# Sums of weight blocks made ahead: twenty sets instead of thirteen, and five of eight pairs as sums in every gate and up product

## The chip, the cores and the metric

One NeuronCore of a Trainium2 chip runs the whole program. The time is the device time of one execution in microseconds (us); less is better. The engines are TensorE (PE; its weight loads are listed as PEld), VectorE (DVE), ScalarE (ACT), GpSimd (POOL) and SyncE (SP, which only issues transfers). Transfers (DMA) move data between HBM and the on-chip memory SBUF, or from HBM to HBM.

## The reference

One layer of an encoder on x (256 tokens x 2048) and mem (256 x 2048), all in f32:

```python
h = rms_norm(x, g_mix); proj = h @ w_in                 # latents for one attention, q/k/v for the other
x = x + concat(out_mla, out_diff) @ w_out               # two kinds of attention heads
hx, hm = rms_norm(x, g_xattn), rms_norm(mem, g_mem)
xo = attention(hx @ w_xq, hm @ w_xk, hm @ w_xv)         # 4 heads into mem
x = x + xo @ w_xo
hf = rms_norm(x, g_ffn)
x = x + (silu(hf @ w_gate) * (hf @ w_up)) @ w_down      # hidden width 5632
return rms_norm(x, g_final)
```

The change concerns the two products hf @ w_gate and hf @ w_up, whose weights have 2048 rows and 5632 columns each.

## The kernel before, in words

**Products.** f32 operands are split in a high part (rounded to fp32r, a cast on ACT) and a low part (the rest, a subtraction on DVE), `split_into`. A product of a 128-row block with 512 columns of weights is three matmuls: high by high, high by low, low by high (`mm`, `mm_late`). Activations (256 tokens, two halves of 128) are the stationary operand, weights the moving one.

**Pairs.** In the wide products (w_out, gate, up, down; `wide_project`) the weights come in pairs: 256 rows by 1024 columns, four blocks of 128 x 512, 1 MB. A pair of kind "P" is used plainly: 8 products, 24 matmuls. A pair of kind "W" is used as sums in Strassen-Winograd fashion, 7 products, 21 matmuls. For that, sums of the activations' blocks are made once (`summed_pair`, the "forms"), and four sums of the weight blocks are needed for each pair: with the blocks stored in the order b0, b1, b2, b3 they are t1 = b1 + b0, t3 = b2 + b0, t2 = t1 + b2, t4 = t2 + b3. Each needed block or sum is split on ACT and DVE. Without sums made ahead, DVE makes the four where they are used (tiles tsum, tsum2). Strings such as 'PPWPWPWW' say the kind of each of the eight pairs of a product, and a tuple beside it the order in which they are used; the third item names a block whose low part is made by an accumulating transfer instead of DVE ("carried").

**Early sets.** `ahead()` is called once for each piece of weights in the projections and pairs before the feed-forward part, and counts these calls as steps: from 0 in the projections of the second attention, through w_out (from 20), the cross-attention (from 36) and w_xo (48 to 51), on into the feed-forward part. An entry ((chunk, 0 for gate or 1 for up, pair), step, own) of `AHEAD` makes the four sums of that pair at that step: two loads of the blocks by SP, four additions on DVE, two stores of the sums to HBM by POOL. With own = 0 the two tiles are taken from the pool act, with own = 1 from a pool of their own (apart). Later `wide_project` finds the set in `made`, loads three of the pair's four raw blocks and the four sums (tile tmade, 1 MB, one buffer), and DVE has no sums to make for that pair.

**Feed-forward part.** A first narrow chunk of 512 columns of gate and up together, then five chunks of 1024 columns; each is a gate product, then an up product (`wide_chunk`), each of eight pairs. After the narrow chunk and chunk 0, after chunks 1 and 2, and after 3 and 4 the down projection of what is there follows (`wide_add`).

**Order.** Every operation is recorded and then ordered by a planner (`Plan.emit`), with a cost for each kind (`Plan.cost`: time on the engine, lag to the result, time of the transfer). It runs its own model of the engines and the transfer queue, derives from it a latest start for each operation, and writes each engine's instructions out in the modelled order. On the chip each engine goes through its list in order and waits by semaphores. An operation's lag may be raised by hand (`.lag += 6.5`), which lets what depends on it come later in the lists. All operations are issued by one helper line, so the profile gives line 244 for all; tiles tell them apart. `wraw` is a raw pair of weights, `wh` and `wl` its split parts, `ahead` the tiles of early sets, `sums` their places in HBM, `acc` and `q` PSUM accumulators.

Of the kernel before, what the change touches and what calls it, by code (L numbers as in the profile page):

```python
# [10 lines left out]
F32 = mybir.dt.float32  # L11
# [4 lines left out]
ALU = mybir.AluOpType  # L16
AX = mybir.AxisListType

P = 128
# [20 lines left out]

NARROW_KINDS, NARROW_ORDER = "PPWPWPPP", (0, 1, 3, 2, 5, 4, 6, 7)
GATE_UP = [
    (('PPWPWPWW', (0, 2, 1, 4, 3, 6, 7, 5), ((0, 1),)),
     ('PPWWWPWW', (0, 2, 3, 1, 4, 6, 7, 5), ((0, 1),))),
    (('PPWPWPWW', (0, 2, 1, 4, 3, 6, 7, 5), ((0, 1),)),
     ('PPWWWPWW', (0, 2, 3, 1, 4, 6, 7, 5), ((0, 1),))),
    (('PPWWWPWW', (0, 2, 3, 1, 4, 6, 7, 5), ((0, 1),)),
     ('PPWWWPWW', (0, 2, 3, 1, 4, 6, 7, 5), ((0, 1),))),
    (('PPWPWPWW', (0, 2, 1, 4, 3, 6, 7, 5), ((0, 1),)),
     ('PPWWWPWW', (0, 2, 3, 1, 4, 6, 7, 5), ((0, 1),))),  # L50
    (('PPWWWPWW', (0, 2, 3, 1, 4, 6, 7, 5), ((0, 1),)),
     ('PPWWWPWW', (0, 2, 3, 1, 4, 6, 7, 5), ((0, 1),))),
]
X2_KINDS = "".join("W" if "W" in k else "P" for k in zip(NARROW_KINDS, *[p[0] for c in GATE_UP for p in c]))

AHEAD = (((0, 1, 2), 2, 0), ((0, 1, 6), 6, 1), ((1, 1, 2), 9, 0), ((1, 1, 6), 11, 0), ((2, 1, 2), 14, 0), ((2, 1, 6), 39, 1), ((3, 1, 2), 40, 0), ((3, 1, 6), 46, 0), ((4, 1, 2), 46, 0), ((4, 1, 6), 46, 1), ((4, 0, 6), 49, 0), ((2, 0, 6), 49, 0), ((4, 0, 2), 50, 0))

OUT_KINDS, OUT_ORDERS = ("PPPPWWWP", "PPPPWWWP"), ((0, 1, 2, 3, 4, 5, 7, 6), (0, 1, 2, 4, 3, 5, 7, 6))  # L60

# [136 lines left out]
class Plan:  # L198
# [64 lines left out]

    def cost(self, engine, method, out, ins, kw):
        if kw.get("accum_op") is not None:
            return 0.6, 4.5, 2.8
        if method == "dma_start":
            size = max(x.cols() for x in out + ins) * 512
            return {"gpsimd": 0.55, "sync": 0.45, "scalar": 0.45}[engine], 2.0 + size / 375e3, size / 381e3
        n = max([x.cols() for x in out[:1]] + ([x.cols() for x in ins[:1]] if "reduce" in method else []))  # L270
        in_psum = bool(ins) and ins[0].tile.whole
        if engine == "tensor":
            t = 0.108 if method == "transpose" else 0.0134 + n / 2400
            return t, t + 0.14, 0.0
        if engine == "gpsimd":
            if method in ("memset", "affine_select", "tensor_copy"):
                t = 0.1 + n * 1.2e-3
            else:
                t = 1.0 if n <= 2 else 1.2
            return t, t + 0.03, 0.0  # L280
        if engine == "vector":
            if n <= 16 and "reduce" not in method:
                t = 0.08
            elif method == "scalar_tensor_tensor":
                t = 0.127 + n * 1.05e-3
            elif method == "tensor_scalar":
                t = 0.129 + n * 1.035e-3 if in_psum else n / 960
            elif method == "tensor_tensor_reduce":
                t = 0.145 + n / 960
            elif method == "tensor_copy":  # L290
                t = n / 960
            else:
                t = 0.068 + n / 960
            return t, t + 0.082, 0.0
        t = 0.044 + 0.855e-3 * n if in_psum else 0.092 + 0.842e-3 * n
        if isinstance(kw.get("scale"), Ref) or isinstance(kw.get("bias"), Ref):
            t += 0.09 if n < 512 else 0.15
        if kw.get("accum_out") is not None:
            t += 0.093
        return t, t + (0.15 if kw.get("accum_out") is not None else 0.08), 0.0  # L300
# [171 lines left out]
def encoder_block(tc: tile.TileContext, a, out):  # L472
    nc = plan = Plan(tc)
# [42 lines left out]
    def act_tile(shape=(P, 4, S), name="act"):  # L516
        return Split(
            act.tile(list(shape), F32R, name=name + "_h", tag="act"),
            act.tile(list(shape), F32R, name=name + "_l", tag="act"),
        )  # L520
# [37 lines left out]
    def project(actT, pieces, before=None, fine=0):  # L558

        accs = [acc_tile() for _ in range(NT)]  # L560
        ncols = pieces[0].shape[2]
        nk = sum(src.shape[1] for src in pieces)
        kt = 0
        for i, src in enumerate(pieces):
            if before is not None:
                before(i)
            ahead()
            for w in weights(src, i < fine):
                x = actT(kt)
                for tt in range(NT):  # L570
                    mm(accs[tt][:, :ncols], x[tt] if isinstance(x, tuple) else x[:, tt * P:(tt + 1) * P], w,
                       start=kt == 0, stop=kt == nk - 1)
                kt += 1
        return accs
# [4 lines left out]
    def nat(name):  # L579
        pool, bufs = nat_pool  # L580
        return pool.tile([P, 512], F32, name=name, tag="nat", bufs=bufs)
# [27 lines left out]
    dram = plan.pool("dram", 1, bass.MemoryType.DRAM)  # L609
    made, steps = {}, [None]  # L610

    def ahead():

        if steps[0] is None:
            return
        for key, at, own in AHEAD:
            if at != steps[0]:
                continue
            src = a[("w_gate", "w_up")[key[1]]][key[0], key[2]]
            x, y = [pool.tile([P, 2, 512], F32, name="ahead", tag=tag)  # L620
                    for pool, tag in ((apart, "ahead" + n) if own else (act, "act") for n in "xy")]
            nc.sync.dma_start(out=x, in_=src[:, 1:3, :]).lag += 6.5
            nc.sync.dma_start(out=y, in_=src[:, 0:4:3, :]).lag += 6.5
            made[key] = d = dram.tile([P, 4, 512], F32, name="sums%d_%d_%d" % key)
            nc.vector.tensor_tensor(out=x[:, 0, :], in0=x[:, 0, :], in1=y[:, 0, :], op=ALU.add)
            nc.vector.tensor_tensor(out=y[:, 0, :], in0=x[:, 1, :], in1=y[:, 0, :], op=ALU.add)
            nc.vector.tensor_tensor(out=x[:, 1, :], in0=x[:, 0, :], in1=x[:, 1, :], op=ALU.add)
            nc.gpsimd.dma_start(out=d[:, 0:4:2, :], in_=x).lag += 3.5
            nc.vector.tensor_tensor(out=y[:, 1, :], in0=x[:, 1, :], in1=y[:, 1, :], op=ALU.add)
            nc.gpsimd.dma_start(out=d[:, 1:4:2, :], in_=y).lag += 3.5  # L630
        steps[0] += 1

    def pair_raw(src, part=False):
# [55 lines left out]
    def wide_project(pairs, src, order, kinds, leave, join, closed=(0, 1), before=None, seed=None, carried=(), sums={}):  # L689
# [6 lines left out]
        for n, i in enumerate(order):  # L696
            stop = n == len(order) - 1
            if before is not None:
                before(n)
            ahead()  # L700
            d = sums.get(i)
            raw = pair_raw(src[i], d is not None)
            if d is not None:
                t = sum_pool[0].tile([P, 4, 512], F32, name="tmade", tag="tmade", bufs=1)
                nc.sync.dma_start(out=t, in_=d).lag += 2.5
            if n == 0 and seed is not None:
                loaded = plan.ops[-1]
                for tt in range(NT):
# [23 lines left out]
            elif sum_pool:  # L732
                t = sum_pool[0].tile([P, 2, 512], F32, name="tsum", tag="tsum", bufs=1)
# [8 lines left out]
            else:  # L742
                b21 = split_blocks(raw[:, 3:4, :])
                t = [soft.tile([P, 512], F32, name="tsum", tag="e", bufs=4) for _ in range(4)]
# [10 lines left out]
            own = i == summed[0], i == summed[-1]  # L755
# [15 lines left out]
    def wide_result(pairs, src, order, kinds, carried=(), sums={}):  # L771

        res = []

        def leave(Q):
            res[:] = [act.tile([P, 2, 512], F32, name=f"res{tt}", tag="act") for tt in range(NT)]
            q1, x, v, y = res[0][:, 0, :], res[0][:, 1, :], res[1][:, 0, :], res[1][:, 1, :]
            nc.scalar.copy(out=q1, in_=Q[1])
            nc.vector.tensor_tensor(out=v, in0=Q[6], in1=q1, op=ALU.subtract)
            nc.vector.tensor_tensor(out=x, in0=Q[5], in1=v, op=ALU.add)  # L780
            nc.vector.tensor_tensor(out=v, in0=v, in1=Q[7], op=ALU.subtract)
            nc.vector.tensor_tensor(out=y, in0=Q[5], in1=v, op=ALU.add)

        def join(tt, oc, acc):
            r = res[tt][:, oc, :]
            nc.vector.tensor_tensor(out=r, in0=acc, in1=r, op=ALU.subtract if (tt, oc) == (1, 0) else ALU.add)

        wide_project(pairs, src, order, kinds, leave, join, carried=carried, sums=sums)
        return res
# [87 lines left out]
    for i in range(8):  # L877
# [8 lines left out]
        for k, w in enumerate(weights(a["w_in_lat"][i], one_by_one,  # L886
# [3 lines left out]
            for tt in range(NT):  # L890
                x = xk[:, tt * P:(tt + 1) * P]
# [227 lines left out]
    for hg in range(2):  # L1119
        t = act_tile(name="mixT")  # L1120
# [141 lines left out]
    for tt in range(NT):  # L1262
        n = nat("xk")
# [6 lines left out]
    for tt in range(NT):  # L1270
        n = nat("xq")
# [19 lines left out]
    for oc in range(4):  # L1291
# [7 lines left out]
        for n in range(2):  # L1299
# [6 lines left out]
            if not plain:  # L1306
                t = act_tile(name="x2T")
# [60 lines left out]
    for gi, (chunks, order) in enumerate(groups):  # L1368
# [6 lines left out]
        src = [a["w_dn"][h, pair0:pair0 + len(hp)] for h in range(2)]  # L1375
# [149 lines left out]
```

## Time and profile before

| | |
|---|---|
| median of 3 runs | 1129.36 us (1128.56 to 1129.73) |
| the profiled execution | 1129.81 us, span 1128.0 us from first to last instruction |
| mean granted TensorE clock | 0.998 |
| early sets: additions on DVE | 52 of 0.68 us (13 sets) |
| loads of made sums (tmade) | 13 of 1 MB |
| bytes moved | 267.53 MB, mean 237 GB/s |

A page of the profile is one execution. Busy shares are averages over the whole span; a matmul that overlaps the next counts as busy, so PE at 99% is read together with the number of matmuls in a stretch. A wait is put down to the event that ended it. In the chain that ended last each row has start, duration and what ran or was waited for. The feed-forward part takes about the second half and more of the span.

### The profile page before, as it was taken

How to read it: one execution, taken by the hardware profiler on the slowest of the kernel's cores; microseconds unless marked ns; L12 is line 12 of the kernel's file. 1: busy time of each engine (PE TensorE's matmuls, PEld its weight loads, DVE VectorE, ACT ScalarE, POOL GpSimd, SP SyncE). 2: the span in 40 equal slices, each digit the busy share in tenths (PEclk: the TensorE clock that was granted, in tenths of full speed). 3: DMA queues.
4: the chain of work that ended last, by engine and by line, in shares of the span. 5: the costliest groups of instructions: out<-in, count | busy, mean ns of one | idle time of the engine just before them, and what ended most of it. 6: DMA issues, size and time to landing. Idle time of an engine off the chain costs nothing.

```text
span 1128.0 us, 14989 instructions
## 1 busy us (share of the span) xinstructions
PE 1117.4 (99%) x5328; PEld 934.3 (83%) x5328; DVE 1040.1 (92%) x1429; ACT 726.0 (64%) x1030; POOL 90.3 (8%) x116
## 2 busy tenths in 40 slices
PE   9999999999999999999999999999999999999997
PEld 7889888888888888888888888888878888888886
DVE  7798889779999899999999999999989999999995
ACT  7756455467775556657776576777656576767752
POOL 5830001000001010000000000000000000000000
PEclk9999999999999999999999999999999999999999
DMA  9745577647676995659657686686566776777543
GB/s 357 261 161 191 187 279 251 240 168 266 234 285 222 360 388 217 206 200 305 223 191 244 219 278 206 247 282 224 189 206 212 257 258 233 279 250 232 219 149 113
DMA packets 48683, 267.53 MB, mean 237 GB/s; under 512 B 5601, under 2 KB 6881, under 8 KB 24289
## 3 DMA queue, kind: packets, MB, share of 16 engines
q1 hardware_dynamic: 40976, 240.46, 59.2%
q0 software_dynamic: 6768, 24.64, 7.4%
q10 hardware_dynamic: 864, 1.47, 0.4%
q8 instruction: 42, 0.69, 0.2%
q14 instruction: 33, 0.26, 0.1%
HBM read 242.96 MB, written 15.73 MB: 229 GB/s over the span
## 4 chain that ended last, share of the span: by engine, by line
PE 93%; DVE 3%; DMA 2%; issue 1%; ACT 0%; SPq 0%; POOLq 0%; POOL 0%; DVEq 0%; ACTq 0%
PE acc L244 69%; PE q L244 16%; PE pt L244 2%; PE psc L244 2%; PE acckv L244 1%; DMA ahead<-in_w_gate 1%; DVE wl L244 1%; PE qT L244 1%; DMA wl<-wraw 1%; PE po L244 1%; PE kT L244 1%; PE pod L244 1%; PE ppt L244 0%; PE wps L244 0%; DVE tsum L244 0%
## 5 line engine op out<-in xcount | busy, mean ns | idle before, releaser
L244 ACT CAST wh<-wraw 128x1024 fp32r<-128x1024 f32 (+2 forms) x401 | 384.1, 967 | 237.3 <-PE acc L244 182.6
L244 DVE TENSOR_TENSOR wl<-wraw,wh 128x1024 fp32r<-128x1024 f32 (+2 forms) x386 | 426.7, 1116 | 51.1 <-ACT wh L244 46.6
L244 ACT CAST wh<-tsum 128x1024 fp32r<-128x1024 f32 (+1 forms) x112 | 112.0, 1005 | 48.8 <-PE acc L244 25.5
L244 DVE TENSOR_TENSOR wl<-tsum,wh 128x1024 fp32r<-128x1024 f32 (+1 forms) x112 | 129.7, 1161 | 3.7 <-ACT wh L244 2.0
L244 PE MATMUL q<-wh,forms_h 128*128 128x512 f32 x270 | 105.5, 391 | 0.2 <-DVE hT_l L244 0.2
L244 PE MATMUL q<-wh,forms_l 128*128 128x512 f32 x270 | 105.5, 391 | 0.0
L244 PE MATMUL acc<-wh,forms_h 128*128 128x512 f32 x261 | 101.9, 391 | 0.0
L244 PE MATMUL acc<-wh,forms_l 128*128 128x512 f32 x261 | 101.6, 389 | 0.0
L244 PE MATMUL acc<-wl,forms_h 128*128 128x512 f32 x261 | 94.8, 389 | 0.0
L244 PE MATMUL q<-wl,forms_h 128*128 128x512 f32 x270 | 93.9, 389 | 0.0
L244 PE MATMUL acc<-wh,x0T_h 128*128 128x512 f32 x224 | 88.6, 397 | 0.0
L244 PE MATMUL acc<-wh,x0T_l 128*128 128x512 f32 x224 | 88.4, 395 | 0.0
L244 PE MATMUL acc<-wl,x0T_h 128*128 128x512 f32 x224 | 87.9, 393 | 0.0
L244 DVE TENSOR_TENSOR tsum<-tsum,wraw 128x512 f32<-128x512 f32 x112 | 76.6, 684 | 0.7
L244 PE MATMUL acc<-wh,hT_l 128*128 128x512 f32 x188 | 73.4, 390 | 0.0
L244 PE MATMUL acc<-wh,hT_h 128*128 128x512 f32 x188 | 73.4, 390 | 0.0
L244 DVE TENSOR_TENSOR tsum<-wraw 128x1024 f32<-128x1024 f32 (+1 forms) x62 | 68.8, 1114 | 3.8 <-DMA wraw<-in_w_dn 2.5
L244 PE MATMUL acc<-wh,x2T_l 128*128 128x512 f32 x176 | 68.7, 390 | 0.0
L244 PE MATMUL acc<-wh,x2T_h 128*128 128x512 f32 x176 | 68.7, 390 | 0.0
L244 PEld LDWEIGHTS q<-wh,forms_h 128*128 128x128 f32 x270 | 50.7, 188 | 11.3 <-DVE hT_l L244 0.9
L244 PEld LDWEIGHTS q<-wl,forms_h 128*128 128x128 f32 x270 | 50.7, 188 | 10.6
L244 PEld LDWEIGHTS q<-wh,forms_l 128*128 128x128 f32 x270 | 50.7, 188 | 10.2
(375 smaller groups left out, 2319.4 us busy)
## 6 DMA issues: line engine op xcount, KB each, us to landing
wraw<-in_w_dn SPq DMA_DIRECT2D x41, 1024.0 KB, 4.7
wraw<-in_w_gate SPq DMA_DIRECT2D x37, 1024.0 KB, 4.8
wraw<-in_w_up SPq DMA_DIRECT2D x30, 1024.0 KB, 5.2
wraw<-in_w_in SPq DMA_DIRECT2D x24, 1024.0 KB, 5.3
wraw<-in_w_out SPq DMA_DIRECT2D x16, 1024.0 KB, 4.8
sums<-ahead POOLq DMA_DIRECT2D x26, 512.0 KB, 7.5
tmade<-sums SPq DMA_DIRECT2D x13, 1024.0 KB, 6.6
ahead<-in_w_up SPq DMA_DIRECT2D x20, 512.0 KB, 7.8
```

The costliest lines, as they stand in the source:

```text
L244: getattr(getattr(self.tc.nc, engine), method)(*[made(x) for x in args], **{k: made(x) for k, x in kw.items()})
```

## The change

Gate takes five of its eight pairs as sums in all five chunks (before: four in chunks 0, 1 and 3). The early sets grow from thirteen to twenty, so that pairs 2 and 6 of every gate and up product are made ahead, and are spread over steps 3 to 50. Six of them (own = 2) are made without SBUF and DVE: SP copies four blocks from HBM to HBM, and POOL issues four accumulating transfers that add the other blocks. The planner's cost of an accumulating transfer now goes by its size (for the size used before it stays as it was), and the lags of early loads, stores and of the loads of made sums are raised.

```diff
 GATE_UP = [
-    (('PPWPWPWW', (0, 2, 1, 4, 3, 6, 7, 5), ((0, 1),)),
-     ('PPWWWPWW', (0, 2, 3, 1, 4, 6, 7, 5), ((0, 1),))),
...
     (('PPWWWPWW', (0, 2, 3, 1, 4, 6, 7, 5), ((0, 1),)),
      ('PPWWWPWW', (0, 2, 3, 1, 4, 6, 7, 5), ((0, 1),))),
...
+] * 5
-AHEAD = (((0, 1, 2), 2, 0), ((0, 1, 6), 6, 1), ((1, 1, 2), 9, 0), ((1, 1, 6), 11, 0), ((2, 1, 2), 14, 0), ((2, 1, 6), 39, 1), ((3, 1, 2), 40, 0), ((3, 1, 6), 46, 0), ((4, 1, 2), 46, 0), ((4, 1, 6), 46, 1), ((4, 0, 6), 49, 0), ((2, 0, 6), 49, 0), ((4, 0, 2), 50, 0))
+AHEAD = (((0, 1, 2), 3, 1), ((0, 1, 6), 5, 0), ((1, 1, 2), 7, 0), ((1, 1, 6), 10, 0), ((2, 1, 2), 11, 2), ((2, 1, 6), 13, 0), ((3, 1, 2), 16, 1), ((3, 1, 6), 18, 0), ((4, 1, 2), 18, 2), ((4, 1, 6), 21, 0), ((4, 0, 6), 30, 2), ((2, 0, 6), 34, 2), ((4, 0, 2), 38, 2), ((0, 0, 6), 40, 2), ((3, 0, 6), 42, 0), ((2, 0, 2), 43, 1), ((1, 0, 6), 47, 0), ((3, 0, 2), 47, 0), ((0, 0, 2), 50, 0), ((1, 0, 2), 50, 0))
...
         if kw.get("accum_op") is not None:
-            return 0.6, 4.5, 2.8
+            size = out[0].cols() * 512
+            return 0.6, 1.7 + size / 188e3, size / 188e3
...
             src = a[("w_gate", "w_up")[key[1]]][key[0], key[2]]
+            made[key] = d = dram.tile([P, 4, 512], F32, name="sums%d_%d_%d" % key)
+            if own == 2:
+                nc.sync.dma_start(out=d[:, 0:2, :], in_=src[:, 1:3, :]).lag += 5.0
+                nc.sync.dma_start(out=d[:, 2:4, :], in_=src[:, 2:4, :]).lag += 5.0
+                for n, b in ((0, src[:, 0, :]), (1, src[:, 0, :]), (2, d[:, 0, :]), (3, d[:, 2, :])):
+                    nc.gpsimd.dma_start(out=d[:, n, :], in_=b, accum_op=ALU.add).lag += 5.0
+                continue
             x, y = [pool.tile([P, 2, 512], F32, name="ahead", tag=tag)
                     for pool, tag in ((apart, "ahead" + n) if own else (act, "act") for n in "xy")]
-            nc.sync.dma_start(out=x, in_=src[:, 1:3, :]).lag += 6.5
-            nc.sync.dma_start(out=y, in_=src[:, 0:4:3, :]).lag += 6.5
+            nc.sync.dma_start(out=x, in_=src[:, 1:3, :]).lag += 9.0
+            nc.sync.dma_start(out=y, in_=src[:, 0:4:3, :]).lag += 9.0
...
-            nc.gpsimd.dma_start(out=d[:, 0:4:2, :], in_=x).lag += 3.5
+            nc.gpsimd.dma_start(out=d[:, 0:4:2, :], in_=x).lag += 5.0
...
-            nc.gpsimd.dma_start(out=d[:, 1:4:2, :], in_=y).lag += 3.5
+            nc.gpsimd.dma_start(out=d[:, 1:4:2, :], in_=y).lag += 5.0
...
-                nc.sync.dma_start(out=t, in_=d).lag += 2.5
+                nc.sync.dma_start(out=t, in_=d).lag += 3.0
```

More of the change, by code (lines that the diff above doesn't have):

```diff
@@ L42 @@
 GATE_UP = [
-    (('PPWPWPWW', (0, 2, 1, 4, 3, 6, 7, 5), ((0, 1),)),
-     ('PPWWWPWW', (0, 2, 3, 1, 4, 6, 7, 5), ((0, 1),))),
-    (('PPWPWPWW', (0, 2, 1, 4, 3, 6, 7, 5), ((0, 1),)),
-     ('PPWWWPWW', (0, 2, 3, 1, 4, 6, 7, 5), ((0, 1),))),
     (('PPWWWPWW', (0, 2, 3, 1, 4, 6, 7, 5), ((0, 1),)),
      ('PPWWWPWW', (0, 2, 3, 1, 4, 6, 7, 5), ((0, 1),))),
[L49 to L53, printed above, removed]
+] * 5
 X2_KINDS = "".join("W" if "W" in k else "P" for k in zip(NARROW_KINDS, *[p[0] for c in GATE_UP for p in c]))
-AHEAD = (((0, 1, 2), 2, 0), ((0, 1, 6), 6, 1), ((1, 1, 2), 9, 0), ((1, 1, 6), 11, 0), ((2, 1, 2), 14, 0), ((2, 1, 6), 39, 1), ((3, 1, 2), 40, 0), ((3, 1, 6), 46, 0), ((4, 1, 2), 46, 0), ((4, 1, 6), 46, 1), ((4, 0, 6), 49, 0), ((2, 0, 6), 49, 0), ((4, 0, 2), 50, 0))
+AHEAD = (((0, 1, 2), 3, 1), ((0, 1, 6), 5, 0), ((1, 1, 2), 7, 0), ((1, 1, 6), 10, 0), ((2, 1, 2), 11, 2), ((2, 1, 6), 13, 0), ((3, 1, 2), 16, 1), ((3, 1, 6), 18, 0), ((4, 1, 2), 18, 2), ((4, 1, 6), 21, 0), ((4, 0, 6), 30, 2), ((2, 0, 6), 34, 2), ((4, 0, 2), 38, 2), ((0, 0, 6), 40, 2), ((3, 0, 6), 42, 0), ((2, 0, 2), 43, 1), ((1, 0, 6), 47, 0), ((3, 0, 2), 47, 0), ((0, 0, 2), 50, 0), ((1, 0, 2), 50, 0))
 OUT_KINDS, OUT_ORDERS = ("PPPPWWWP", "PPPPWWWP"), ((0, 1, 2, 3, 4, 5, 7, 6), (0, 1, 2, 4, 3, 5, 7, 6))
@@ L619, in ahead @@
             src = a[("w_gate", "w_up")[key[1]]][key[0], key[2]]
+            made[key] = d = dram.tile([P, 4, 512], F32, name="sums%d_%d_%d" % key)
[5 more added lines that the diff above has]
+                continue
             x, y = [pool.tile([P, 2, 512], F32, name="ahead", tag=tag)
                     for pool, tag in ((apart, "ahead" + n) if own else (act, "act") for n in "xy")]
-            nc.sync.dma_start(out=x, in_=src[:, 1:3, :]).lag += 6.5
-            nc.sync.dma_start(out=y, in_=src[:, 0:4:3, :]).lag += 6.5
-            made[key] = d = dram.tile([P, 4, 512], F32, name="sums%d_%d_%d" % key)
+            nc.sync.dma_start(out=x, in_=src[:, 1:3, :]).lag += 9.0
+            nc.sync.dma_start(out=y, in_=src[:, 0:4:3, :]).lag += 9.0
             nc.vector.tensor_tensor(out=x[:, 0, :], in0=x[:, 0, :], in1=y[:, 0, :], op=ALU.add)
```

## Prediction

> **What bounds the kernel now.** I read the page first (span, busy shares, chain), then the waits of PE alone, then the chain in order of time, then the span cut into stretches of 20 us, and last the groups with their shapes kept apart.
>
> ```profile
> span 1128.0 us, 14989 instructions
> PE 1117.4 (99%) x5328; PEld 934.3 (83%) x5328; DVE 1040.1 (92%) x1429; ACT 726.0 (64%) x1030; POOL 90.3 (8%) x116
> PE 93%; DVE 3%; DMA 2%; issue 1%; ACT 0%; SPq 0%; POOLq 0%; POOL 0%; DVEq 0%; ACTq 0%
> ```
>
> TensorE works from end to end, and 93% of the chain that ended last is its own matmuls. So the time is the number of matmuls times the time of one, and a few waits. All of these waits are in the next view (PE's own):
>
> ```profile
> PE wps L244 <- DVE warm L244: 1.2, 1, 1.2
> PE acc L244 <- DMA wl<-wraw: 0.7, 1, 0.7
> PE po L244 <- DVE val_l L244: 0.4, 1, 0.4
> PE q L244 <- DVE hT_l L244: 0.2, 1, 0.2
> PE po L244 <- ACT val_h L244: 0.2, 1, 0.2
> ```
>
> Without the start (1.2) that is 1.5 us, at three places. The chain says where, and gives the time of a matmul:
>
> ```profile
> 380.93 13.23 DMA ahead<-in_w_gate
> 404.03 2.66 PE po L244 x20
> ...
> 481.05 1.21 DVE tsum L244
> 482.92 1.20 PE q L244 x4
> ...
> 574.32 5.67 PE acc L244 x25
> ...
> 829.38 9.09 DMA wl<-wraw
> ```
>
> 25 matmuls of 512 columns in 5.67 us are 0.227 us each. The three waits end at 404 (behind early loads of the made sums, which DVE waited for), at 483 (behind DVE, in the first gate chunk) and at 838 (behind an accumulating transfer of the down projection). In stretches of 20 us (columns: busy time of PE, PEld, DVE, ACT, POOL, each with its count; then clock, DMA share, GB/s):
>
> ```profile
> 120.00:140.00 20.00, 20.00 (x98) 16.61 (x98) 15.67 (x24) 9.65 (x14) 1.61 (x2) 1.00 0.74 263
> 140.00:160.00 20.00, 20.00 (x94) 16.55 (x93) 15.86 (x22) 8.35 (x9) 1.38 (x2) 1.00 0.78 287
> 200.00:220.00 20.00, 20.00 (x93) 16.56 (x93) 14.49 (x21) 8.12 (x9) 1.37 (x2) 1.00 0.60 215
> 220.00:240.00 20.00, 20.00 (x105) 17.00 (x105) 15.31 (x31) 12.52 (x28) 0.00 (x0) 1.00 0.55 204
> 380.00:400.00 20.00, 20.00 (x104) 16.74 (x103) 19.69 (x39) 11.92 (x26) 2.06 (x3) 1.00 1.02 409
> 400.00:420.00 20.00, 19.47 (x100) 16.10 (x99) 18.80 (x27) 11.29 (x17) 4.92 (x7) 1.00 1.01 402
> 480.00:500.00 20.00, 19.76 (x89) 15.81 (x88) 19.93 (x24) 11.68 (x14) 0.00 (x0) 1.00 0.57 211
> 820.00:840.00 20.00, 19.35 (x85) 15.69 (x84) 19.31 (x25) 12.82 (x15) 0.84 (x1) 1.00 0.65 188
> 980.00:1000.00 20.00, 20.00 (x90) 16.57 (x89) 19.82 (x24) 15.02 (x19) 0.84 (x1) 1.00 0.81 268
> ```
>
> PE loses 0.53, 0.24 and 0.65 us at the three places, 1.42 together. DVE is full from about 480 on (19.8 to 19.9 of 20) and has 4.1 to 5.5 us free in each of the four early stretches shown. The transfers are full only from 380 to 420 (shares 1.02 and 1.01).
>
> **The change part by part.** Rows for DVE and ACT, shapes kept apart (busy us, mean ns | idle before):
>
> ```profile
> L244 DVE TENSOR_TENSOR wl<-wraw,wh 128x1024 fp32r<-128x1024 f32 x299 | 362.4, 1224 | 44.8 <-ACT wh L244 40.3 <-PE q L244 2.7
> L244 DVE TENSOR_TENSOR wl<-tsum,wh 128x1024 fp32r<-128x1024 f32 x100 | 121.5, 1218 | 3.0 <-ACT wh L244 2.0 <-PE acc L244 0.6
> L244 DVE TENSOR_TENSOR tsum<-tsum,wraw 128x512 f32<-128x512 f32 x112 | 76.6, 684 | 0.7
> L244 DVE TENSOR_TENSOR tsum<-wraw 128x1024 f32<-128x1024 f32 x50 | 60.9, 1217 | 3.2 <-DMA wraw<-in_w_dn 2.5 <-DMA wraw<-in_w_gate 0.7
> L244 DVE TENSOR_TENSOR wl<-wraw,wh 128x512 fp32r<-128x512 f32 x71 | 48.5, 683 | 1.0 <-ACT wh L244 1.0
> L244 DVE TENSOR_TENSOR ahead<-ahead 128x512 f32<-128x512 f32 x52 | 34.9, 684 | 0.3
> L244 DVE TENSOR_TENSOR wl<-tmade,wh 128x1024 fp32r<-128x1024 f32 x26 | 31.6, 1217 | 0.1
> L244 ACT CAST wh<-wraw 128x1024 fp32r<-128x1024 f32 x314 | 327.5, 1052 | 197.4 <-PE acc L244 157.3 <-issue 17.1 <-PE q L244 4.3
> ```
>
> **Matmuls.** A plain pair is 8 products of 3 matmuls, 24; a pair as sums 7 products, 21. The gates of chunks 0, 1 and 3 go from four to five such pairs (pair 3 is new); all other products stay, and so do the forms of x2, since pair 3 was wanted as sums by the up products already. 3 x 3 = 9 matmuls x 0.227 = 2.04 us less on the path that sets the end.
>
> **DVE and ACT in these gates.** On DVE a plain pair costs 2 x 1.224 = 2.45 us; as sums made in place 1.224 + 1.217 + 1.218 + 0.683 + 2 x 0.684 + 1.218 = 6.93; with sums made before, 1.224 + 1.217 + 0.683 + 1.217 = 4.34. Each of these three gates had 4 plain (one block's 1.224 is done by a transfer) and 4 sums in place: 36.3 us. It gets 3 plain, 3 in place and 2 made: 35.6. So DVE falls by 0.7 us a gate, as PE does (40.8 to 40.1): no gain in slack, and no loss. Chunk 2's gate saves 6.93 - 4.34 = 2.6. ACT pays 3 x 1.052 plus a half-size cast against 2 x 1.052, under 2 us a gate; 64% busy, it hides that. That five such pairs, two of them made, can be fed is shown by chunk 4, whose gate and up have that form already: the stretch 980 to 1000 lies in it, with PE at 20.00.
>
> **The early sets.** Twenty instead of thirteen, six by transfers alone, so DVE makes fourteen: 4 x 0.684 = 2.74 us more in all. More important is where: eight of DVE's sets come at steps 3 to 21 instead of five at steps 2 to 14, 8.2 us more DVE before 260, beside the 4.3, 4.1, 5.5 and 4.7 us free in the four stretches. From step 39 to 50 eight of DVE's sets become six: 5.5 us less DVE just ahead of the waits at 404 and 483. If the cover of an early add is gone, it costs its 0.68 us on PE.
>
> **Transfers and queues.**
>
> ```profile
> sums<-ahead POOLq DMA_DIRECT2D x26, 512.0 KB, 7.5
> ahead<-in_w_up SPq DMA_DIRECT2D x20, 512.0 KB, 7.8
> wl<-wraw POOLq DMA_DIRECT2D x15, 512.0 KB, 7.0
> ahead<-in_w_gate SPq DMA_DIRECT2D x6, 512.0 KB, 14.9
> ```
>
> Those are the page's issues (KB each, median us to landing); next, a wait of SP's own queue (total, times, longest), and the first and last issue of two kinds of load:
>
> ```profile
> SPq L244 <- DMA sums<-ahead: 11.3, 2, 9.8
> L244 SPq DMA_DIRECT2D wraw<-in_w_gate x40: 327/328/328, 452.0 to 968.0; - x40
> L244 SPq DMA_DIRECT2D ahead<-in_w_gate x6: 398/580/1469, 378.0 to 390.2; - x6
> ```
>
> SP gets 12 copies from HBM to HBM, 2 more early loads and 7 more loads of made sums (each made pair moves 768 + 1024 KB instead of 1024). The weight loads behind them are late only by the issue (0.33 us each). SP already waited 11.3 us for stores of made sums, and PE did not wait there, so the prefetch covers such a wait. The new readers sit earlier: chunk 0's gate reads two sets, and the gate loads begin at 452.0. The last early loads were issued at 390.2 and land after 14.9 us, so adds and store (7.5) have some 40 us; I take nothing.
>
> POOL gets 24 accumulating transfers and 2 more stores, issue only, at 8% busy. No accumulation between two HBM places is in the trace. The nearest row is the accumulation in SBUF, 7.0 us for 512 KB; an add here is half as large. I take 7.0 for one, so that a set takes copy 7.8 plus three adds in a row, about 29 us: nobody waits for it before the feed-forward part. Bounds: nothing (done in the shadow), or, on the bad side, POOL holding back its next instruction:
>
> ```profile
> 342.81 1.08 POOL L244 TENSOR_TENSOR rstdm<-rstdm,mhalf 128x2 f32<-128x2 f32 x1 [46.55 <-DVE rstdm L244]
> L244 DVE TENSOR_SCALAR xk<-acc,rstdm x2: 740/742/744, 351.2 to 351.9; 128x512 f32<-128x512 f32 x2
> ```
>
> rstdm is done at 343.9 and used at 351.2, 7.3 us later: one add's landing (7.0) ahead of it on POOL is covered, a second one is not. The Trainium skill says in "DMA: Bandwidth & Descriptors", section "Anatomy of one DMA", that the DMA engines do not wait on semaphores: a wait is sat out on the issuing sequencer ahead of the dispatch. The trace agrees in kind (POOL sat 46.55 us ahead of rstdm). By that section's fit of 2.0 us plus bytes over 436 GB/s an add of 256 KB would take an estimated 2.6 us, and the sum would stay as it is.
>
> **Waits kept or lost.** The wait at 404 hangs on loads that landed after some 14.9 us, under full transfers; 47, 47, 50, 50 are still four sets there, so it stays or shrinks. The one at 483 stood behind the sums of gate chunk 0's second pair, now made before (2.6 us less DVE), but the third pair is a new one in place. Between nothing and 0.53 + 0.24 = 0.77, I take half, 0.4. The one at 838 has other causes and stays.
>
> **Sum.** -2.04 - 0.4 = -2.4 us. Against the profiled execution's own 1129.81 us (span 1128.0, 1.8 around it) that is 1127.4; the median of the runs, 1129.36, lies 0.45 below it, so 1126.9.
>
> **The rivals.** *All three waits go*: 2.04 + 1.42 = 3.5, 1125.9. For it: less DVE ahead of two of them. Against: the third is not touched.
>
> *New waits eat the gain*: the order of every engine is laid out anew, and DVE, in order, can sit on an early load with softmax or rope work behind it. For it: 8.2 us more adds before 260. Against: no wait of PE in those stretches now. Two or three such waits of 0.5 us: 1129.36 - 2.04 + 1.2 = 1128.5.
>
> *Slower, by the transfers between 340 and 420*: two sets by accumulation fall at steps 38 and 40, just ahead of the stretch where the DMA share is 1.02. The six early loads of gate weights there landed after 14.9 instead of 7.8 us, 7.1 us later, and cost PE 0.53; if that delay comes once more and DVE sits on all of it, 1129.36 - 2.04 + 7.1 = 1134.4. It decides from 4.3 us of new waiting on. The Trainium skill speaks for it ("DMA: Bandwidth & Descriptors", "Issuing engines are not separate DMA queues": transfers of all issuing engines interleave on the same 16). Against: eight sets lie between steps 39 and 50 now, seven after.
>
> *Slower, by POOL*: two landings stacked ahead of rstdm, 14.0 - 7.3 = 6.7 us late at xk, if PE's banks run out: 1134.0.
>
> **How the numbers follow.** 0.2% is 2.3 us, about what a measurement of this kernel can tell from no change: faster lies below 1127.1, slower above 1131.6. Forecast 0.46 (its own range 1126.3 to 1127.3, of which I count 0.06 above 1127.1), all waits gone 0.13, gain eaten 0.29, slower 0.12 (transfers 0.07, POOL 0.05). Faster 0.46 + 0.13 - 0.06 = 0.53; same 0.29 + 0.06 = 0.35; slower 0.12. The range leaves the slower cases out above (1130.8 is 1127.3, the matmuls alone, with 3.5 us of new waits) and reaches down to 1125.0, the 1125.9 less the 0.8 by which the lowest run lies below the median, rounded down.
>
> **What would show it.** Right: PE's records fall by about nine, PE full through gates 0, 1 and 3, DVE's early adds 56, no PE wait above 0.5 us near 404 and 483. Wrong: a PE wait on sums or tmade, rstdm or x1Tr late with POOL behind an accumulation, DVE idle before an early add in 100 to 260 with PE idle just after, or early loads landing later than 15 us.

## The result and the profile after

The changed kernel takes 1139.38 us (median; 1138.39 to 1140.1) against 1129.3 for the kernel before: a ratio of 1.009 (95% interval 1.0078 to 1.0102), 10 us slower. The forecast of 1126.9 and its range were wrong. The page of the changed kernel (line 236 is its helper line, as 244 was before):

```profile
span 1137.8 us, 15044 instructions
...
PE 1119.7 (98%) x5319; PEld 933.9 (82%) x5319; DVE 1037.0 (91%) x1427; ACT 730.3 (64%) x1036; POOL 112.8 (10%) x142
...
PE 87%; DMA 6%; DVE 5%; issue 2%; ACT 1%; POOLq 0%; POOL 0%; DVEq 0%; ACTq 0%
...
L236 DVE TENSOR_TENSOR tsum<-wraw 128x1024 f32<-128x1024 f32 (+1 forms) x58 | 63.8, 1106 | 13.3 <-DMA wraw<-in_w_out 12.4
...
wraw<-in_w_out SPq DMA_DIRECT2D x16, 1024.0 KB, 8.3
```

PE has nine matmuls less, as intended, but its share of the chain fell from 93% to 87%, and DMA's rose from 2% to 6%. The new name is `wraw<-in_w_out`: the raw weights of w_out, the projection that runs just before the cross-attention. DVE sat 12.4 us idle for them. Before, the page's row for these loads and for DVE's sums was:

```profile
L244 DVE TENSOR_TENSOR tsum<-wraw 128x1024 f32<-128x1024 f32 (+1 forms) x62 | 68.8, 1114 | 3.8 <-DMA wraw<-in_w_dn 2.5
...
wraw<-in_w_out SPq DMA_DIRECT2D x16, 1024.0 KB, 4.8
```

A stage begins with the first matmul on its activations (mixT for w_out, mT for the cross-attention's keys); the number ahead of "to" is its start. First before, then after:

```profile
L244 PE MATMUL acc<-wh,mixT_h x64: 388/389/476, 239.6 to 310.5; 128*128 128x512 f32 x64
L244 PE MATMUL acc<-wh,mT_h x64: 388/389/479, 326.9 to 401.9; 128*128 128x512 f32 x64
```

```profile
L236 PE MATMUL acc<-wh,mixT_h x64: 387/389/478, 240.2 to 316.4; 128*128 128x512 f32 x64
L236 PE MATMUL acc<-wh,mT_h x64: 388/389/484, 339.9 to 414.8; 128*128 128x512 f32 x64
```

Cut in this way at every stage (us, from one profiled execution each):

| stage | before | after | difference |
|---|---|---|---|
| start to w_out | 239.6 | 240.2 | +0.6 |
| w_out | 87.3 | 99.7 | **+12.4** |
| cross-attention up to w_xo | 79.6 | 79.9 | +0.3 |
| w_xo, narrow chunk, chunk 0 | 150.3 | 149.2 | -1.1 |
| first down projection | 64.4 | 64.5 | +0.1 |
| chunks 1 and 2 | 163.1 | 162.4 | -0.7 |
| their down projection | 85.8 | 84.8 | -1.0 |
| chunks 3 and 4 | 163.0 | 162.3 | -0.7 |
| the rest | 94.8 | 94.7 | -0.1 |

So from w_xo on 3.5 us were won; w_out alone lost 12.4. Stretches of w_out (columns as in the prediction): of before, then of after.

```profile
239.60:326.90 87.30, 87.30 (x401) 72.34 (x400) 80.86 (x121) 61.19 (x105) 3.56 (x6) 1.00 0.66 242
```

```profile
240.20:339.90 99.70, 92.05 (x401) 73.62 (x400) 83.16 (x126) 61.91 (x105) 13.44 (x18) 0.97 0.85 278
300.00:305.00 5.00, 4.20 (x19) 3.12 (x18) 5.00 (x7) 2.71 (x5) 0.00 (x0) 1.00 0.32 96
305.00:310.00 5.00, 3.46 (x15) 2.25 (x13) 5.00 (x10) 4.92 (x11) 0.00 (x0) 1.00 0.95 346
320.00:325.00 5.00, 0.58 (x4) 0.15 (x2) 2.07 (x4) 1.04 (x3) 0.29 (x1) 0.82 1.04 358
325.00:330.00 5.00, 5.00 (x12) 3.98 (x13) 4.96 (x6) 3.48 (x6) 0.00 (x0) 0.50 1.01 360
```

The same 401 matmuls; 7.65 us of the loss are idle, 4.75 are matmuls that took longer. PE nearly stands still from 320 to 325 and then gets half its clock (0.50): 12 matmuls in 5 us. The chain in order of time (start, us, what) and POOL's own instructions in that stretch say why; both of the kernel after.

```profile
287.96 10.55 DMA wraw<-in_w_out
298.53 0.07 DVE tsum L236
...
313.35 9.49 DMA wraw<-in_w_out
322.93 0.10 DVE tsum L236
```

```profile
285.55 1.77 POOL L236 DMA_DIRECT2D sums<-in_w_gate  x2 [36.76 <-DMA sums<-in_w_gate]
294.56 0.80 POOL L236 DMA_DIRECT2D sums<-sums  x1 [7.25 <-DMA sums<-in_w_gate]
310.17 1.66 POOL L236 DMA_DIRECT2D sums<-in_w_gate  x2 [14.80 <-DMA sums<-in_w_gate]
...
317.27 0.83 POOL L236 DMA_DIRECT2D sums<-sums  x1 [4.60 <-DMA sums<-in_w_gate]
317.80 2.49 POOL L236 DMA_DIRECT2D mn<-in_mem  x4
```

Twice a raw pair takes 9.5 to 10.6 us to land, DVE waits for it, and PE waits for DVE. Beside it POOL issues the adding transfers of the sets of steps 30 and 34, sits in order on their landings (the brackets: idle before, and for what), and only then issues the four loads of mem (`mn`, 512 KB each), all within 2.49 us. Before, these stood apart (the first and the last of the four):

```profile
245.96 0.60 POOL L244 DMA_DIRECT2D mn<-in_mem  x1
...
295.74 0.53 POOL L244 DMA_DIRECT2D mn<-in_mem  x1 [12.32 <-PE acc L244]
```

How much of the transfer engines the additions hold is in the queues of one stretch, 290 to 295 of after (packets, MB, and the time of the packets as a share of 16 engines; q0 is POOL's queue, which carries only additions here, q1 SP's, with weight loads):

```profile
q0 software_dynamic: 197, 0.36, 62.3%
q1 hardware_dynamic: 84, 0.63, 41.4%
```

0.623 x 16 x 5 us / 0.36 MB is 138 engine-us a MB for POOL's queue against 53 for SP's. The Trainium skill says in "DMA: Bandwidth & Descriptors", section "SWDGE vs HWDGE vs iDMA", that each DMA engine takes turns between its internal queues, and that GpSimd's and SP's transfers sit in different ones. The shares agree with that: the slow additions hold more than half of the engines while the weight load waits its turn; single turns are not in these rows.

### The profile page after: what moved, and what is told of

Read it like the earlier page. It is cut to its first block, busy times and chain, and to the rows that moved or that the text cites. A ratio compares the mean times of both kernels' runs of the same rounds, so it can differ in the third digit from the quotient of the medians.

```text
span 1137.8 us, 15044 instructions
## 1 busy us (share of the span) xinstructions
PE 1119.7 (98%) x5319; PEld 933.9 (82%) x5319; DVE 1037.0 (91%) x1427; ACT 730.3 (64%) x1036; POOL 112.8 (10%) x142
## 2 busy tenths in 40 slices
DMA packets 55579, 287.72 MB, mean 253 GB/s; under 512 B 6352, under 2 KB 7632, under 8 KB 31184
## 3 DMA queue, kind: packets, MB, share of 16 engines
q10 hardware_dynamic: 864, 1.47, 0.4%
## 4 chain that ended last, share of the span: by engine, by line
PE 87%; DMA 6%; DVE 5%; issue 2%; ACT 1%; POOLq 0%; POOL 0%; DVEq 0%; ACTq 0%
PE acc L236 62%; PE q L236 17%; DMA wraw<-in_w_out 4%; PE pt L236 2%; DVE wl L236 2%; DMA wraw<-in_w_xv 2%; PE acckv L236 1%; PE psc L236 1%; PE qT L236 1%; PE po L236 1%; DVE tsum L236 1%; DVE ahead L236 1%; ACT wh L236 1%; PE kT L236 1%; PE wps L236 0%
## 5 line engine op out<-in xcount | busy, mean ns | idle before, releaser
L236 ACT CAST wh<-tsum 128x1024 fp32r<-128x1024 f32 (+1 forms) x104 | 103.8, 1001 | 42.1 <-DVE tsum L236 23.3
L236 DVE TENSOR_TENSOR wl<-tsum,wh 128x1024 fp32r<-128x1024 f32 (+1 forms) x104 | 120.1, 1156 | 3.5 <-PE acc L236 1.8
L236 PE MATMUL q<-wh,forms_h 128*128 128x512 f32 x282 | 110.1, 390 | 0.8 <-ACT wh L236 0.8
L236 PE MATMUL q<-wh,forms_l 128*128 128x512 f32 x282 | 110.1, 390 | 0.0
L236 PE MATMUL q<-wl,forms_h 128*128 128x512 f32 x282 | 99.2, 392 | 5.3 <-DVE wl L236 5.3
L236 PE MATMUL acc<-wh,forms_h 128*128 128x512 f32 x246 | 96.3, 391 | 0.0
L236 PE MATMUL acc<-wh,forms_l 128*128 128x512 f32 x246 | 96.1, 391 | 0.0
L236 PE MATMUL acc<-wh,x0T_l 128*128 128x512 f32 x224 | 87.9, 393 | 0.0
L236 DVE TENSOR_TENSOR tsum<-wraw 128x1024 f32<-128x1024 f32 (+1 forms) x58 | 63.8, 1106 | 13.3 <-DMA wraw<-in_w_out 12.4
L236 DVE TENSOR_TENSOR tsum<-tsum,wraw 128x512 f32<-128x512 f32 x104 | 71.0, 683 | 0.5
L236 POOL DMA_DIRECT2D wl<-wraw x15 | 12.8, 856 | 520.1 <-ACT wl L236 375.0
```

What stands on the lines that cost most here:

```text
L236: getattr(getattr(self.tc.nc, engine), method)(*[made(x) for x in args], **{k: made(x) for k, x in kw.items()})
```

## The experiments

The theory was that the accumulated sets of steps 30 and 34 cost the time in w_out by their bytes, which are dear because they are added, and so crowd out the loads of weights. A rival is that POOL is held by the accumulations, and the mem loads behind them come late and at once. Another is that the planner's new order, or the fifth pair in the gates, costs it. All times below stand against 1129.2 to 1129.5 us of the kernel before, run beside each; "w_out" is the length of that stage in the profiled execution, 87.3 before.

**The two halves of the change.** The gates alone:

```diff
 # the kernel before
-GATE_UP = [ ... chunks 0, 1, 3: gate 'PPWPWPWW' ... ]
+GATE_UP = [ gate 'PPWWWPWW', up 'PPWWWPWW' ] * 5
```

> The kernel before with one part of the change: five of eight pairs as sums in every gate; the thirteen early sets, their steps and all lags stay. Two theories put the loss of the changed kernel (10 us) in the w_out stage, where its PE stands still (4.58 us at 325 and three times about 0.9 us before it): T1, the transfers from HBM to HBM fill the DMA engines and delay the w_out weights; T2, POOL sits behind the accumulations and lets the four loads of mem go in one burst at 318. By both this kernel is 2.0 us faster than before (9 matmuls of 0.227 us), at 1127.3. T3, the five pairs ask too much of DVE in the feed-forward part: slower than before, by 2 to 10 us.

Measured 1132.73 (ratio 1.0034, 1.0022 to 1.0047); w_out 87.4, so the loss is not made here. But w_xo to chunk 0 takes 155.0 instead of 150.3. PE's waits:

```profile
PE acc L236 <- DVE forms_l L236: 2.3, 1, 2.3
```

In chunk 0 DVE can't make five pairs' sums in place besides the forms; with two sets made ahead, as in the change, it could (149.2). Chunk 0 left as before:

```diff
-] * 5
+] with chunk 0's gate 'PPWPWPWW' as before, and chunks 1 to 4 as in the change
```

> The kernel before with five pairs as sums in the gates of chunks 1 and 3 alone; chunk 0's gate keeps four, the thirteen early sets stay. If chunk 0 alone cannot feed a fifth pair with sums in place (its first gate, behind the narrow chunk, lost 4.6 us when all three gates were changed without made sums): 6 matmuls less, 1.4 us, and up to 1 us at the following down projection, 1127.0 to 1128.5. If the gates of chunks 1 and 3 cannot be fed either: 1129.4 and more.

1129.19 (1.0000, 0.9991 to 1.0009). Six matmuls less are 1.36 us; the profiled span is 0.9 us shorter, and the runs can't tell it from nothing. Now the change without the two sets that stood in w_out:

```diff
-AHEAD = (... ((4, 0, 6), 30, 2), ((2, 0, 6), 34, 2), ...)
+AHEAD = (... both left out ...)
```

> The changed kernel without the two sets at steps 30 and 34 (pair 6 of the gates of chunks 4 and 2 gets its sums in place). T1 and T2: the w_out stage, from its first matmul to the first one on mem, goes from 99.7 back to 87 to 88 us and the time to 1127 to 1129. T3, or a loss spread over all six sets: w_out improves but the time stays above 1133.

1132.16 (1.0027, 1.0017 to 1.0037), w_out 88.8: the 12.4 us fall to 1.5. The time is still 2.7 us above before, more than was expected: besides w_out 1.1 us lie ahead of it, and the 1.2 us that the chunks win are lost again in the second down projection (0.7) and after the last chunk (0.5). The opposite test gives the kernel before just these two transfers:

```diff
 # the kernel before
+AHEAD += (((0, 0, 6), 30, 2), ((1, 0, 6), 34, 2)), with the code for own = 2
```

> The kernel before with nothing but two accumulated sets added, at steps 30 and 34 (pair 6 of the gates of chunks 0 and 1, which needs no sums in place then); all else stays. T1: w_out takes 3 to 10 us longer than the 87.3 before and the time is 1132 to 1139. If it takes the changed kernel's other sets as well to make the wait (T6: a queue of late transfers from step 18 on), w_out stays within 1.5 us and the time within 1 us of before.

1139.15 (1.009, 1.0076 to 1.0104), w_out 100.0. Two sets at these two steps, with no other move, make a loss as large as the whole change's. The fifth pair falls as its cause.

**What it is about them.** On these two sets I took away the adding (plain copies of the same bytes in the same order; the sums are then not sums), the lateness of the mem loads, and both:

```diff
-nc.gpsimd.dma_start(out=d[:, n, :], in_=b, accum_op=ALU.add)
+nc.gpsimd.dma_start(out=d[:, n, :], in_=b)          # "copies", planned at the same cost
-load.after(mixed, False)                              # mem loads: not before mixed
+load.after(diffed, False)                             # "mem early": ahead of the accumulations on POOL
```

> The kernel before with the two accumulated sets at steps 30 and 34 (w_out 100.0 us there against 87.3), and the four loads of mem ahead of the accumulations in POOL's list. T1, the sets' own transfers delay the w_out weights: w_out stays at 94 us or more. T2, the late burst of 2 MB for mem behind POOL's waits does it: w_out falls to 90 us or less. Both together: between.

> The same kernel (before with two sets at 30 and 34, mem loads behind them) with the adding transfers issued as plain copies in the same order (leaves out the additions). T1 in its sharp form, the read of the destination doubles a packet's time (178 ns against 84) and that is what fills the transfers: w_out falls to 90 to 94 us. T2: w_out stays above 96, as POOL waits for landings all the same.

> The kernel before with two sets at steps 30 and 34, made by plain copies instead of adding transfers, and with the mem loads ahead of them (leaves out the additions). The two sizes found one at a time, each off w_out's 12.7 us of excess: 4.9 for mem early, 6.0 for the copies. If they are separate bytes in one crowded stretch they add up: excess 1 to 4 us, w_out 88 to 91. If each only helps because it breaks the same last wait, they do not add: w_out stays at 92 to 94.

| two sets in the kernel before | median | ratio (95%) | w_out over 87.3, profiled execution |
|---|---|---|---|
| added, mem late | 1139.15 | 1.009 (1.0076 to 1.0104) | 12.7 |
| added, mem early | 1136.58 | 1.0067 (1.0053 to 1.008) | 7.8 |
| copies, mem late | 1134.1 | 1.0046 (1.0032 to 1.0059) | 6.7 |
| copies, mem early | 1130.77 | 1.0015 (1.0006 to 1.0025) | 1.5 |

In w_out each alone takes off 4.9 or 6.0 us, both 11.2: they add up. These lengths are from one profiled execution each, and of the first and the third kernel that was the slowest of four runs (1142.03 and 1135.96). By the medians the four lie 9.7, 7.4, 4.9 and 1.4 us above the kernel before: mem early takes off 2.3 or 3.5, the copies 4.8 or 6.0, both 8.3. So both effects stand, the adding is the larger, and their sizes are good to a few us. With mem early the squares of mem on ACT move into w_out too (262 to 277 instead of 344 to 355), so that edit shifts a little more than the loads. The page's row for DVE's sums shows the wait go (in the order of the table; the last number is the idle time and its cause):

```profile
L244 DVE TENSOR_TENSOR tsum<-wraw 128x1024 f32<-128x1024 f32 (+1 forms) x60 | 66.4, 1111 | 19.6 <-DMA wraw<-in_w_out 12.4
```

```profile
L244 DVE TENSOR_TENSOR tsum<-wraw 128x1024 f32<-128x1024 f32 (+1 forms) x60 | 66.5, 1113 | 14.3 <-DMA wraw<-in_w_out 8.7
```

```profile
L244 DVE TENSOR_TENSOR tsum<-wraw 128x1024 f32<-128x1024 f32 (+1 forms) x60 | 66.5, 1113 | 13.9 <-DMA wraw<-in_w_out 6.5
```

```profile
L244 DVE TENSOR_TENSOR tsum<-wraw 128x1024 f32<-128x1024 f32 (+1 forms) x60 | 66.5, 1113 | 9.6 <-DMA wraw<-in_w_gate 3.4
```

The price of the adding is in the two kernels with mem early, in the stretch 280 to 340, where POOL's queue carries nothing but the two sets; first with additions, then with copies:

```profile
q0 software_dynamic: 1152, 2.10, 25.9%
```

```profile
q0 software_dynamic: 640, 2.10, 14.0%
```

The same bytes hold the engines 1.85 times as long: 118 against 64 engine-us a MB. The additions went in packets of 2 KB with a median of 178 ns, the copies in packets of 4 KB with 159 ns; plain 2 KB packets on SP's queue in the same stretch took 84 ns, so it is not the size of the packets alone. Last, the two sets with hardly any bytes: the chain of waits on POOL stays, but each transfer is 16 columns wide, into places that nobody reads, and the two pairs take raw blocks for their sums:

```diff
-out=d[:, n, :], in_=b
+out=d[:, n, :16], in_=b[:, :16]      # likewise the copies, all planned at the full cost
```

> The kernel before with the two sets' twelve transfers at steps 30 and 34 kept in the same places of SP's and POOL's lists, with the same dependences, but 16 columns wide instead of 512 and into places that nobody reads; the two pairs then load raw blocks where their sums would be (leaves the sums out). T2 alone, POOL's waits and the late burst of mem: w_out at 90 us or more. T1, bytes and packets of the sets: w_out at 87 to 89.

1131.04 (1.0015, 1.0006 to 1.0024), w_out 88.8. The mem loads still come in one burst (305.9 to 307.6; in the kernel above with two full sets 314.8 to 316.4). The order, a shorter chain of waits and a burst 9 us earlier thus cost 1.5 us; the rest needs the sets' own bytes. A burst as late as 314.8 without these bytes was not tried. With this kernel the new order falls as a cause as well, and the theory and its rival are each half right: slow bytes, and the mem loads that the additions push into them.

The same two edits on the changed kernel:

> The changed kernel with its four accumulating transfers of each of the six sets issued as plain copies, same sources, places, waits and order of every engine (leaves out the additions). T1: a packet of 2 KB takes about 84 ns instead of 178, so the transfers are full for less long: waits of PE in w_out fall by a third to two thirds, 1131 to 1136. T2: POOL still sits on four landings in a row and the loads of mem still go in one burst: waits of PE in w_out change by less than 2 us, 1137 to 1139.

> The changed kernel with the four loads of mem placed ahead of the accumulations of steps 30 and 34 in POOL's list, instead of behind them. T2: the wait of 4.58 us at 325 and the cold clock after it go, 1130 to 1133. T1: the transfers of the two sets remain on the w_out loads: 1136 to 1139.

Copies (here in all six sets): 1131.25 (1.0014, 1.0005 to 1.0023), w_out 92.5. Mem early: 1137.84 (1.0076, 1.0063 to 1.009), w_out 96.6. Of the 12.4 us in w_out the adding is 7.2 and the mem loads' place 3.1; by the medians they are 8.3 and 1.7 of the whole excess of 10.1 (the profiled execution of the copies was the slowest of ten, 1132.75).

**The two sets made by DVE instead,** at the same steps:

```diff
-((4, 0, 6), 30, 2), ((2, 0, 6), 34, 2)
+((4, 0, 6), 30, 0), ((2, 0, 6), 34, 0)
```

> The changed kernel with the two sets at steps 30 and 34 made on DVE through SBUF instead of by accumulation. Adding transfers are the cause (T1, to which the plain copies point: 92.5 us for w_out instead of 99.7): w_out takes 89 to 93 us and the time is 1129 to 1133. Any set at these steps is the cause, whatever its kind (T4): DVE is full there too (19.2 of 20 us), so w_out stays at 96 us or more and the time above 1135.

1141.26 (1.0104, 1.0089 to 1.012). w_out is nearly cured (90.2), but the next stage, the cross-attention's keys, takes 34.8 instead of 25.3. PE's waits, and the chain:

```profile
PE pt L236 <- DVE xk L236: 8.5, 1, 8.5
```

```profile
341.58 15.91 DMA wraw<-in_w_xq
```

The same number of bytes (287.72 MB in both kernels), now through stores and loads, crowds the stretch behind: a weight load took 15.9 us, and PE waited 8.5 us at xk. rstdm, made on POOL, started at 363.2 instead of 342.8, but POOL had then been idle and waiting for DVE's part of it:

```profile
363.17 0.71 POOL L236 TENSOR_TENSOR rstdm<-rstdm,mhalf 128x2 f32<-128x2 f32 x1 [4.33 <-DVE rstdm L236]
```

So POOL didn't hold it back, as the prediction's POOL rival would have it. DVE was late, and on the chain the weight load lies ahead of DVE; how much of the 8.5 us is due to that load alone was not taken apart.

**Other places for the two sets.** Into the first attention:

```diff
-((4, 0, 6), 30, 2), ((2, 0, 6), 34, 2)
+((4, 0, 6), 1, 2), ((2, 0, 6), 2, 2)
```

> The changed kernel with the sets of steps 30 and 34 moved, still by accumulation, to steps 1 and 2, whose transfers SP issues at about 84 us, ahead of a stretch in which the transfers were nearly idle (share 0.07 from 100 to 120 in the kernel before). T1: contention costs only where weights are being loaded: w_out goes back to 87 to 88 us, the time to 1126 to 1128. If an accumulated set costs the same wherever it stands (T5), the loss moves along: 1135 and more.

1130.46 (1.0006, 0.9997 to 1.0015): w_out 87.9, but w_out begins at 243.7 instead of 240.2. Into the feed-forward part:

```diff
-((4, 0, 6), 30, 2), ((2, 0, 6), 34, 2)
+((4, 0, 6), 78, 2), ((2, 0, 6), 62, 2)
```

> The changed kernel with the two sets moved to steps 62 and 78, in the feed-forward part (chunk 0's gate and the first down projection), where the DMA share is 0.6 to 0.8. T1: w_out back to 87 to 89 us; the weights there have four raw buffers, so PE loses 0 to 4 us in the feed-forward part: 1126 to 1131. T5: 1135 and more.

1129.62 (1.0007, 0.9998 to 1.0017), w_out 90.0: no loss that the runs can tell, and no gain either, as 2.5 us are won from w_xo on and w_out loses 2.7. In the versions that follow all accumulated sets stand in the feed-forward part, and DVE's sets at the steps, and with the lags, that they had before:

```diff
+GATE_UP as in the change; AHEAD: DVE's sets at steps 2 to 14 and 39 to 50, own = 2 at
+  nine sets: 62 78 90 98 106 114 122 130 138     (11 by DVE)
+  three:     62 70 78                            (13 by DVE)
+  six:       62 70 78 84 122 130                 (11 by DVE)
+  four:      62 78 122 130                       (11 by DVE)
```

> A version put together from the findings: five pairs as sums in every gate and twenty sets, but the steps before the feed-forward part hold eleven sets made on DVE at the steps of the kernel before (chunk 0's and chunk 1's gate sets among them), and the other nine are accumulated within the feed-forward part, one in every 8 to 16 steps from 62 on. If contention costs only where weights have a short lead (T1): w_out and all before it as in the kernel before, 3 us less in the feed-forward part, 1125 to 1127. If adding transfers cost PE in the feed-forward part too, some 1 us for each set: 1132 and more.

> A version from the findings: five pairs as sums in every gate; thirteen sets on DVE at the steps of the kernel before, chunk 0's two gate sets among them; three more accumulated at steps 62, 70 and 78 (chunk 0's products and the first down projection), none while the gates and ups of chunks 1 to 4 load their weights, where nine such sets took 4.9 us. Expected span by the stages measured in the other runs: 406.4 to the cross-attention's end, 149.4, 64.4, 162.4, 85, 162.3, 94.7, together 1124.6, so 1126 us, 3 us faster than before. If one of the three sets collides with chunk 0's loads: 1128 or more.

> Five pairs as sums in every gate; eleven sets on DVE at early steps (the eleven that gave chunk 0's part 149.4 us), six accumulated at steps 62, 70, 78, 84, 122 and 130 (chunk 0's products and the two down projections), three sets not made at all. Expected span from the stages measured so far: 239.6, 87.3, 25.3, 54.0, 149.4, 64.4, 162.4, 85.5, 162.5, 94.7, together 1125.1, so about 1126.6 us, 0.2% faster than before. If the sets at 70 and 84 meet chunk 0's and the down projection's loads, 1 to 2 us more and no difference that can be told.

> The same with four accumulated sets, at 62, 78, 122 and 130; five sets are not made and their sums are made in place. If DVE in chunks 3 and 4 can stand that (chunks 1 and 3 could, with four unmade pairs in a gate): the same 1126 to 1127 us. If not, 1 to 4 us more in the last gate and up products.

| accumulated sets in the feed-forward part | median | ratio (95%) | where it is lost |
|---|---|---|---|
| nine | 1131.19 | 1.0017 (1.0008 to 1.0025) | chunks 1 and 2: 168.0 (163.1) |
| six | 1130.87 | 1.0019 (1.001 to 1.0028) | first down projection: 68.2 (64.4) |
| four | 1129.77 | 1.0003 (0.9994 to 1.0012) | chunks 3 and 4: 164.4 (163.0) |
| three | 1129.35 | 1.0002 (0.9993 to 1.0011) | w_xo to chunk 0: 152.1 (150.3) |

The lengths in the last column are again of the profiled execution (the kernel before in brackets); that of the six was the slowest of its ten runs, 1133.86. w_out is 87.3 to 87.4 in all four. The six have a wait of another kind; PE's waits:

```profile
PE acc L236 <- DMA wl<-wraw: 4.1, 3, 1.9
```

`wl<-wraw` are the accumulating transfers that make a carried block's low part, also on POOL's queue: here PE waits for those. None of the versions was faster than the kernel before.

## Why the prediction was wrong, point by point

**Right: the matmuls.** Nine records less; chunks 1 and 2, and 3 and 4, each 0.7 us shorter, 3 x 0.227 as summed.

**Right, and more than forecast: the waits.** The waits at 483 and 838 are gone; the one at 404 is still there (`po`, 0.7, at 417 now). The sum took 0.4 us off for the first two and kept the third; in fact the down projection after chunk 2 became 1.0 us shorter, and w_xo to the end won 3.5. That this is the figure of the rival "all three waits go" is luck: the wait at 404 lies ahead of w_xo and stayed, and the matmuls with the two waits that went are 2.04 + 0.24 + 0.65 = 2.9; the other 0.6 us were not traced. PE's list of after:

```profile
PE q L236 <- DVE wl L236: 5.3, 3, 4.4
...
PE q L236 <- ACT wh L236: 0.8, 1, 0.8
PE acc L236 <- DVE wl L236: 0.8, 1, 0.8
PE po L236 <- DVE val_l L236: 0.7, 1, 0.7
```

The rows of `q` and `acc` lie in w_out; from w_xo on PE waits for nothing that the list has.

**Nearly right: DVE's early additions.** 56 of 0.68 us, and the stages before w_out became 0.6 us longer in all. The slack covered most of them, but not all: just behind the start of w_out PE waited 0.5 us for val_l (`pod`), and on the chain an early addition (240.55, 0.68 us) stands just ahead of val_l.

**Failed: the step "Transfers and queues".** It put the accumulated sets at nothing because "nobody waits for it before the feed-forward part". That is true of the sets, and beside the point: others wait, for the transfer engines and for POOL's queue. It said that the weight loads come late "only by the issue (0.33 us each)"; those of w_out landed after 8.3 us instead of 4.8 (medians), and w_out became 12.4 us longer. Three things in it were off:
- The price. 7.0 us was taken for one addition's landing, from a row with twice the bytes. The medians in the trace of after are 8.1, 9.1 and 11.5 us:

```profile
sums<-in_w_gate POOLq DMA_DIRECT2D x8, 256.0 KB, 8.1
sums<-sums POOLq DMA_DIRECT2D x12, 256.0 KB, 9.1
sums<-in_w_up POOLq DMA_DIRECT2D x4, 256.0 KB, 11.5
mn<-in_mem POOLq DMA_DIRECT2D x4, 512.0 KB, 13.1
```

Latency was the wrong unit, too. An addition holds the engines 1.85 times as long as a copy of the same bytes, and with copies 7.2 of the 12.4 us were back.
- POOL "issue only". Each set is a chain, and POOL sits in order on its landings. The row that the prediction took for agreement on this (46.55 us ahead of rstdm) is a wait ahead of arithmetic; ahead of transfers it is the 14.80 and 4.60 us above. The step asked what stands behind (rstdm, with 7.3 us to spare) but stopped there; the four mem loads stand behind too, and these are bytes. Their place cost 1.7 to 3.1 us here, and 2.3 to 5.2 in the kernel with the two sets alone (by the medians and by w_out).
- The place. The rival on transfers looked at 340 to 420, where the share was 1.02 already, and gave it 7.1 us and a chance of 0.07. The cross-attention, which fills most of that stretch, became 0.3 us longer. The sets of steps 30 and 34 begin at 278, in w_out, whose share had been 0.66: room on average. But PE there lives on raw pairs that land in 4.8 us, and when two of them took 10, DVE and PE ran dry.

**The rival by POOL** (two landings ahead of rstdm) is not what happened in the change: rstdm began at 356.7 with POOL idle 4.6 us for its operand, so it was late because w_out was. Nor is it what happened with the DVE-made sets, where POOL was idle ahead of rstdm too.

## What to carry to other kernels

A transfer that nobody reads for long still isn't free: cost it in engine time (its bytes by the price of its kind, here 1.85 times a copy's for an addition), lay that beside the landing times that the running stage lives on, and list everything that the issuing engine's queue holds behind its waits, transfers included. A mean DMA share of 0.66 says nothing on whether the next load may come 5 us later. Test a bundle of many moves by the two moves that lie in the tightest stage: here 2 of them made a loss as large as all 20.

## What the runs showed of the hardware that was not expected

A gap of PE is paid twice. After 4.42 us without a matmul the next ones of 512 columns started 0.43 us apart instead of 0.227, for 5 us (kernel after):

```profile
324.88 0.80 PE L236 MATMUL q<-wl,forms_h 128*128 128x512 f32 x1 [4.42 <-DVE wl L236]
325.47 0.63 PE L236 MATMUL acc<-wh,forms_h 128*128 128x512 f32 x1
...
329.74 0.53 PE L236 MATMUL acc<-wh,diffT_l 128*128 128x512 f32 x1
330.11 0.39 PE L236 MATMUL acc<-wh,diffT_h 128*128 128x512 f32 x1
```

That is 12 x 0.2 = 2.4 of the 4.75 us by which w_out's matmuls took longer; the rest was not taken apart (the ends of matmuls are modelled). The three gaps of 0.7 to 0.8 us between 300 and 310 left the clock at 1.00. The Trainium skill, "TensorE: Matmul & The Clock Gate", section "What's actually happening", puts the fall to half behind an idle window of about 3.4 us. The gap of 4.42 us agrees. In the gates-alone kernel a gap of 2.29 us was enough, and the fall came 1.1 us after PE had resumed:

```profile
508.79 0.50 PE L236 MATMUL acc<-wh,forms_l 128*128 128x512 f32 x1 [2.29 <-DVE forms_l L236]
...
509.91 0.63 PE L236 MATMUL q<-wh,forms_l 128*128 128x512 f32 x1
510.34 0.63 PE L236 MATMUL q<-wh,forms_h 128*128 128x512 f32 x1
```

Other traces of this case narrow it. The first row is of the changed kernel with mem early, where the granted clock is 0.71 from 270 to 275; the second of the one with the two sets in the first attention, where it is 1.00 from 220 to 230:

```profile
270.54 0.50 PE L236 MATMUL q<-wh,forms_h 128*128 128x512 f32 x1 [1.57 <-ACT wh L236]
```

```profile
223.95 0.63 PE L236 MATMUL psc<-dT_h 128*128 128x256 f32 x3 [1.47 <-ACT dT_h L236]
```

So these shorter gaps do not fit the 3.4 us of the Trainium skill, and the measurement decides: here a gap of 1.57 us was already followed by half the clock, one of 1.47 us was not. In the clock records of the traces half the clock lasts 3.41 us after gaps of 1.50 to 3.26 us, 6.83 us after 3.64 and 4.42, and 10.24 us after 8.20 and 8.53. Two gaps are not a limit; other gaps beside them may count too.
